# Attention with the heads of chunks 1 and 0 alternating, one sequence of other products, and x3 joined before its sum

## The chip, the cores and the metric

The kernel runs on one core of a Trainium2 chip. A core has a tensor engine (PE, matrix products and transposes, with a weight load PEld before each), a vector engine (DVE), a scalar engine (ACT), a GpSimd engine (POOL) and a sync engine (SP) on whose queue nearly all transfers are issued. Each runs its own list of instructions in order; they meet at semaphores. The metric is the device time of one execution in microseconds, as the median of several runs.

## The reference

A trunk of two layers over 2048 tokens of width 1024, in 32-bit floats. The first layer is a pooling mixer. Keys and values come from its result x2, once. The second layer, where the change lies, is:

```python
h = rms_norm(x, b_norm[j])
q, z = jnp.split(h @ b_w_in[j], 2, axis=-1)
o = stick_breaking_attention(q, k_sh, v_sh)      # 16 heads of 64
x = x + (o * jax.nn.silu(z)) @ b_w_out[j]        # x3
x = x + (p[i] @ ple_w[i]) * jax.nn.sigmoid(x @ ple_gate_w[i])
```

The attention weight of key s for query t is sigmoid(logit) times the product of (1 - sigmoid) over the keys between s and t: a running product along the keys, taken from the last key back, for all keys before the query.

## The kernel before, in words

A product in full precision is made of three passes: each operand is stored as a rounded high part and the rest, and high*high, high*rest and rest*high are summed in PSUM (`piecewise`, L882 to L890; L885, L887 and L889 are its three matmuls).

The tokens are four chunks of 512. The first part of the program (to 1364.5 us of the profile) does the first layer for chunks 0 to 3 in turn, and stores queries, keys and values by chunk in HBM, x2 as floats, and its two parts for chunks 0 to 2. The second part is attention, and the products that remain lie beside it.

Attention goes in slots. A slot (c, h, kc) is one head h, the queries of chunk c against the keys of chunk kc; it has four steps, one for each 128 queries. Slots run for c = 3, 2, 1, 0, in each for all 16 heads, in each for kc = c down to 0. A slot with kc = c is a diagonal one, whose four score tiles are 128, 256, 384 and 512 keys wide; the others are full. So chunk 3 has 64 slots, chunk 2 has 48, chunk 1 has 32 and chunk 0 has 16. Step n does three things for three different slots, in the loop at L1035: `turn`, transposes of the running products that were made six steps ago (L841), which ACT copies as high part (L844) and DVE completes by a subtraction (L845); `front`, the scores of this step (L816, L817), sigmoid on ACT (L820) and the running product as a scan on DVE (L825 diagonal, L828 full); `gather`, the product with the values of what was turned two steps ago (L853, L854).

The other products come from a generator, `filler`, of which each step takes `rate` matmuls (L1054 to L1057). During chunk 3's slots it is `gate_z` for chunks 3, 2, 1, 0: z = silu(x2 @ wz) to HBM, 192 matmuls for a chunk. During the slots of chunk c it is then `post(c + 1)`: the output product of the chunk just done, sum to x3 (L947), x3 in two parts (L951 on ACT, L952 on POOL), the gate product and that with the embedding p, and for each of eight tiles of 128 channels sigmoid (L974), multiplication (L978), the two parts of x3 added (L979, on POOL while attention runs, L980), four transposes (L986) and the store. 768 matmuls lie beside 256 steps of chunk 3, 432 beside 192, 128 and 64 steps. At the end of a chunk's heads what is left of the generator is run out, and a new one starts with a new rate (L1068 to L1075). `post(0)` runs last, alone: the tail.

`soon(k, fn)` puts work k steps later in the order. After a pair of heads is done, `gated` (L859) adds the end values, multiplies by z on POOL (L866); `pair_up` (L892) makes the two parts of it that the output product reads (`og`, L897, L898).

Most of the order is that of the source. A scheduler places the instructions on the engines and chooses buffers from the pools: 10 tiles for queries, keys and values, 18 for the pairs that products read, 6 for stored weights, 2 PSUM banks each for scores, turned tiles, sums and dense products.

## Time and profile before

| | |
|---|---|
| median of 3 runs | 2768.99 us (2768.77 to 2770.73) |
| the profiled execution | 2768.39 us |
| its span, first to last instruction | 2765.4 us |
| instructions | 39537 |
| granted clock of PE | 0.999 |

A row of a group names line, engine, operation, the tile written and those read, then count, busy time and mean duration. A row of the waits says who waited for whom, for how many microseconds in total, how many times, and the longest. A row of the windows has the stretch and its length, then for each engine that worked its busy time and number of instructions, then the granted clock of PE, the share of the DMA engines and GB/s. A row of the timeline has start and duration in microseconds; in brackets stands how long the engine was idle before it, and what ended that. Matmuls are pipelined: one of 512 columns shows about 0.39 us, and the next starts 0.23 after it.

### The profile page before, as it was taken

To read this page: it belongs to the slowest core of one execution; us is meant where nothing else is said; L and a number is where in the kernel's file an instruction comes from. 1 tells how busy PE (TensorE), PEld (TensorE's weight loads), DVE (VectorE), ACT (ScalarE), POOL (GpSimd) and SP (SyncE) were. 2 spreads that over 40 slices of the span, in tenths; PEclk is the share of its full clock that TensorE was granted. 3 is DMA by queue.
4 is the path that set the end of the run, shared out by engine and by line. 5 is a ranking of instruction groups with operands and counts; after the bars stand their busy time and mean duration, and the time that the engine had idled before them with its cause. 6 is when DMAs were issued, how large, how long until landed. Compare 5 with 4: busy or idle time off the path is not lost. (4 is left out here: it accounts for less than half of the span.)

```text
span 2765.4 us, 39537 instructions
## 1 busy us (share of the span) xinstructions
PE 2725.7 (99%) x13715; PEld 2260.4 (82%) x13715; DVE 1956.0 (71%) x2573; ACT 1385.5 (50%) x2801; POOL 873.7 (32%) x695
## 2 busy tenths in 40 slices
PE   9999999999999999999999999999999999999999
PEld 7888888888888888888888888887887778888877
DVE  6766535655357544565499999999999988996632
ACT  5444532445234542345356566666666655664521
POOL 2574338642475325753121111111110011112220
PEclk9999999999999999999999999999999999999999
DMA  8664696747946479445678565555555566668765
GB/s 293 236 196 171 218 325 204 225 148 253 347 148 227 163 249 318 136 145 170 191 254 278 180 217 170 169 161 178 169 159 162 159 200 200 188 204 264 249 209 160
DMA packets 335835, 573.21 MB, mean 207 GB/s; under 512 B 32462, under 2 KB 166638, under 8 KB 335636
## 3 DMA queue, kind: packets, MB, share of 16 engines
q1 hardware_dynamic: 330186, 563.03, 63.5%
q10 hardware_dynamic: 5450, 7.66, 0.9%
q8 instruction: 108, 1.77, 0.3%
q14 instruction: 91, 0.75, 0.1%
HBM read 430.01 MB, written 132.19 MB: 203 GB/s over the span
## 5 line engine op out<-in xcount | busy, mean ns | idle before, releaser
L844 ACT CAST at<-psa 128x512 fp32r<-128x512 f32 (+3 forms) x640 | 334.1, 522 | 478.4 <-PE psa L841 459.6
L536 PE MATMUL psd<-wpair,x 128*128 128x512 f32 x2304 | 544.0, 393 | 0.0
L828 DVE TENSOR_TENSOR_SCAN pp<-kap,pp,zeros 128x512 f32<-128x512 f32 x384 | 512.9, 1336 | 3.1 <-ACT kap L820 2.4
L536 PEld LDWEIGHTS psd<-wpair,x 128*128 128x128 f32 x2304 | 428.2, 188 | 86.2
L845 DVE TENSOR_TENSOR at<-psa,at 128x512 fp32r<-128x512 f32 (+3 forms) x640 | 381.0, 596 | 88.0 <-ACT at L844 84.9
L841 PE MATMUL psa<-ident,pp 128*128 128x128 f32 x2176 | 347.0, 275 | 17.2 <-DVE at L845 15.5
L820 ACT ACTIVATE kap<-psl 128x512 f32<-128x512 f32 (+3 forms) x640 | 344.9, 539 | 15.1 <-PE psl L817 12.0
L841 PEld LDWEIGHTS psa<-ident,pp 128*128 128x128 f32 x2176 | 262.9, 140 | 93.0 <-DVE at L845 38.8
L816 PE MATMUL psl<-kk,qa 128*128 128x512 f32 (+3 forms) x640 | 281.4, 440 | 0.0
L854 PE MATMUL pso<-at,vv 128*128 128x512 f32 (+3 forms) x640 | 235.1, 367 | 0.0
L817 PE MATMUL psl<-kk,qb 128*128 128x512 f32 (+3 forms) x640 | 233.0, 364 | 0.0
L853 PE MATMUL pso<-at,vv 128*128 128x512 f32 (+3 forms) x640 | 232.7, 364 | 0.0
L825 DVE TENSOR_TENSOR_SCAN pp<-kap,ahead 128x128 f32<-128x128 f32 (+3 forms) x256 | 219.8, 859 | 5.8 <-ACT kap L820 4.1
L131 PE MATMUL psd<-xp,wpair 128*128 128x512 f32 x512 | 201.9, 395 | 1.3 <-ACT xp L269 0.8
L132 PE MATMUL psd<-xp,wpair 128*128 128x512 f32 x512 | 200.5, 392 | 0.0
L133 PE MATMUL psd<-xp,wpair 128*128 128x512 f32 x512 | 200.1, 391 | 0.0
L113 DVE SCALAR_TENSOR_TENSOR wpair<-wraw,gains,wpair 128x512 fp32r<-128x512 f32 x192 | 169.7, 905 | 36.8 <-ACT wpair L112 36.1
L923 POOL TENSOR_TENSOR zr<-zr,sgz 128x512 f32<-128x512 f32 x32 | 58.8, 1836 | 368.2 <-ACT sgz L922 311.3
L112 ACT ACTIVATE wpair<-wraw,gains 128x512 fp32r<-128x512 f32 x192 | 135.0, 720 | 59.0 <-PE psd L536 32.3
L108 POOL TENSOR_TENSOR wpair<-wraw,wpair 128x512 fp32r<-128x512 f32 x99 | 145.5, 1485 | 59.7 <-ACT wpair L106 59.7
L853 PEld LDWEIGHTS pso<-at,vv 128*128 128x128 f32 x640 | 120.2, 188 | 26.9 <-ACT at L844 0.2
L854 PEld LDWEIGHTS pso<-at,vv 128*128 128x128 f32 x640 | 120.3, 188 | 25.9
(211 smaller groups left out, 5402.4 us busy)
## 6 DMA issues: line engine op xcount, KB each, us to landing
kk<-kd SPq DMA_DIRECT2D x320, 128.0 KB
vv<-vd SPq DMA_DIRECT2D x160, 256.0 KB
wraw<-in_w_kv_dram SPq DMA_DIRECT2D x128, 256.0 KB
wpair<-wzd SPq DMA_DIRECT2D x64, 512.0 KB
wpair<-wod SPq DMA_DIRECT2D x64, 512.0 KB
wpair<-wgd SPq DMA_DIRECT2D x64, 512.0 KB
wpair<-wu SPq DMA_DIRECT2D x48, 512.0 KB
wpair<-wi SPq DMA_DIRECT2D x36, 512.0 KB
```

The costliest lines, as they stand in the source:

```text
L131: T.matmul(ps, wst(units, kt, 0, c0), acts[kt][:, 0], start=(begin and kt == order[0]), stop=False)
L536: T.matmul(pss2[i], ck["x2"][kt][:, xh, tk], wst(ws, kt, wh, 0, W5), start=(kt == 0 and xh == 0 and wh == 0), stop=(kt == KT - 1 and wh == 1))
L816: T.matmul(ps[:, :w], qa[:, qs], kk[:, :w], start=True, stop=False)
L817: T.matmul(ps[:, :w], qb[:, qs], kk[:, :w], start=False, stop=True)
L820: A.activation(out=kp[:, r0:], in_=ps[:, :w], func=AF.Sigmoid, scale=-1.0)
L825: V.tensor_tensor_scan(out=pp[:, r0:][:, ::-1], data0=kp[:, r0:][:, ::-1], data1=ahead[:, r0:][:, ::-1], initial=1.0, op0=ALU.mult, op1=AL ...
L828: V.tensor_tensor_scan(out=pp[:, ::-1], data0=kp[:, ::-1], data1=zeros.to_broadcast([P, W5]), initial=st["carry"][j], op0=ALU.mult, op1=AL ...
L841: T.transpose(pt[:, j * P : (j + 1) * P], pp[:, r0 + kt * P : r0 + (kt + 1) * P], ident)
L844: A.copy(out=at[:, 0, cs], in_=pt[:, cs])
L845: V.tensor_tensor(out=at[:, 1, cs], in0=pt[:, cs], in1=f(at[:, 0, cs]), op=ALU.subtract)
L853: T.matmul(po[:, cs], vv[:, kt, :], at[:, 0, cs], start=(st["diag"] and kt == 0), stop=False)
L854: T.matmul(po[:, cs], vv[:, kt, :], at[:, 1, cs], start=False, stop=(st["last"] and kt == 3))
```

## The change

1. The slots run as (1, h, 1), (1, h, 0), (0, h, 0) for each head, then all of chunk 2, then all of chunk 3. Where a slot has the keys of the slot before, it takes its key and value tiles and loads none. Since two chunks are in work at once, each has its own tile for the sum of a pair of heads.
2. The generator is one for all of attention: z of chunks 0, 1, 2, then `post(0)`, z of chunk 3, `post(1)`, `post(2)`; `post(3)` is the tail. Its rate has two values, one to step 208 and one after, and full steps get 1.2 times the share of diagonal ones. Twenty matmuls are left over for the end of the loop.
3. x2's parts are stored for chunk 3 too, and `gate_z` reads them from HBM for every chunk; those of chunk 0 are loaded ahead of the last step of the first part.
4. A pair of heads whose z isn't there yet is gated later.
5. In `post`, POOL adds the two parts of x3 at the start of a tile's gate product (`xw`), DVE adds that after its multiplication, and the tile's transposes follow two steps later in place of one tile later. In the tail this takes one of DVE's three operations a tile away. p is loaded and turned in two halves within the output products.

Two places show what it moves. PE, where the first attention stage ends. Before, steps 257 to 259, the first of chunk 2 (`psl` scores, `pso` with the values, `psa` turned):

```order
L817 MATMUL psl<-kk,qb 128x128
L853 MATMUL pso<-at,vv 128x512
L854 MATMUL pso<-at,vv 128x512
L841 MATMUL psa<-ident,pp 128x128 x4
L816 MATMUL psl<-kk,qa 128x256
L817 MATMUL psl<-kk,qb 128x256
```

Now, steps 208 and 209, where z of chunk 2 ends and `post(0)` begins (`xz` is x2, `og` the gated heads):

```order
L822 MATMUL psl<-kk,qb 128x512
L899 MATMUL psd<-xz,wpair 128x512
L901 MATMUL psd<-xz,wpair 128x512
L858 MATMUL pso<-at,vv 128x512
L859 MATMUL pso<-at,vv 128x512
L846 MATMUL psa<-ident,pp 128x128 x4
L821 MATMUL psl<-kk,qa 128x512
L822 MATMUL psl<-kk,qb 128x512
L897 MATMUL psd<-xz,wpair 128x512
L899 MATMUL psd<-xz,wpair 128x512
L901 MATMUL psd<-xz,wpair 128x512
L897 MATMUL psd<-og,wpair 128x512
```

The dense products (`psd`) go on through the change of work; before, ten steps had none.

DVE and PE at an output tile. Before, on DVE, a tile's last sum in chunk 2, whose transposes PE has twelve steps (of one scan each) further on:

```order
L825 SCALAR_TENSOR_TENSOR pp<-kap_12823,ahead 128x512
L898 TENSOR_TENSOR og<-os,og 128x512
L845 TENSOR_TENSOR at<-psa,at 128x512
L828 SCALAR_TENSOR_TENSOR pp<-kap_12820,pp,zeros 128x512
L980 TENSOR_TENSOR sg<-sg,x_19035 128x512
```

Now, on DVE, the first tile of chunk 0, at step 275, and on PE its transposes, after the scores of step 277:

```order
L833 SCALAR_TENSOR_TENSOR pp<-kap_12854,pp,zeros 128x512
L1005 TENSOR_TENSOR sg<-psd,sg 128x512
L912 TENSOR_TENSOR og<-os,og 128x512
L1006 TENSOR_TENSOR sg<-sg,xw 128x512
L850 TENSOR_TENSOR at<-psa,at 128x512
L833 SCALAR_TENSOR_TENSOR pp<-kap_12855,pp,zeros 128x512
```

```order
L822 MATMUL psl<-kk,qb 128x128
L899 MATMUL psd<-x_17857,wpair 128x512
L901 MATMUL psd<-x_17857,wpair 128x512
L897 MATMUL psd<-x_18027,wpair 128x512
L1011 MATMUL psao<-ident,sg 128x128 x4
L858 MATMUL pso<-at,vv 128x512
```

The sum now follows its multiplication on the same engine with no POOL instruction between, and PE comes to the tile two steps after it.

The diff, cut to what the steps touch:

```diff
-                if s + 1 < NSUB:
-                    nc.sync.dma_start(out=x2p[s][o], in_=f(pr))
+                nc.sync.dma_start(out=x2p[s][o], in_=f(pr))
...
-                early["q"] = load_q(NSUB - 1, 0)
-                early["k"] = [load_k(NSUB - 1, 0), load_k(NSUB - 2, 0)]
+                early["q"] = load_q(1, 0)
+                early["k"] = [load_k(1, 0), load_k(0, 0)]
+                early["x"] = [load_x2(0, o) for o in range(KT)]
...
                 def gated():
+                    if (c, h2) not in gates:
+                        soon(2, gated)
+                        return
+                    soon(3, finished)
                     zt = t2.tile([P, W5], F32, tag="zt", name="zt", bufs=1)
...
+                def finished():
+                    assert len(outs[c]) == h2
+                    outs[c].append(os)
+
...
                     soon(3, gated)
-                    soon(6, lambda: outs[c].append(os))
...
                 T.matmul(ps, wst(units, kt, 1, c0), acts[kt][:, 0], start=False, stop=(kt == n - 1))
+                if behind:
+                    behind(kt)
                 yield
...
-            xs = chunk[c]["x2"] if c == NSUB - 1 else []
-            for o in range(len(xs), KT):
-                pr = pair("xz")
-                nc.sync.dma_start(out=f(pr), in_=x2p[c][o])
-                xs.append(pr)
+            xs = early.pop("x")
...
-                yield from piecewise(ps, wz, xs, 0)
+                def behind(kt):
+
+                    early.setdefault("x", []).append(load_x2(c + 1, kt))
+
+                yield from piecewise(ps, wz, xs, 0, behind if o == KT - 1 and c < 2 else None)
...
                     nc.sync.dma_start(out=zd[c][o], in_=zr)
+                    gates.add((c, o))
 
                 soon(1, silu)
-                if c == 0:
-                    pair_up(NSUB - 1)
+                if c < 3:
+                    pair_up(0)
+                if c == 2 and o < 2:
+                    pair_up(1)
 
         POSTZ = 8 * 24
-        POST = 8 * 24 + 8 * 31 + 2
+        POST = 8 * 24 + 8 * 31
...
-            pin = t2.tile([P, 4, PLE], F32, tag="pin", name="pin", bufs=1)
-            nc.sync.dma_start(out=pin, in_=p[1, 0, c * W5 : (c + 1) * W5, :].rearrange("(j q) n -> q j n", q=P))
-            x3, og = [], ogs[c]
+            x3, og, pt_ = [], ogs[c], []
+            assert len(outs[c]) == 8
...
                 wo = stored(wod[o])
+                if o in (2, 5):
+                    pin = t2.tile([P, 4, P], F32, tag="pin", name="pin", bufs=1)
+                    nc.sync.dma_start(out=pin, in_=p[1, 0, c * W5 : (c + 1) * W5,
+                                                     len(pt_) * P : (len(pt_) + 1) * P].rearrange("(j q) n -> q j n", q=P))
...
-            pt_ = []
-            for k in range(2):
...
-            yield
+                if o < 2 and 0 < c < NSUB - 1:
+                    pair_up(c + 1)
+                if o in (4, 6):
+                    k = len(pt_)
...
+                    pt_.append(pr)
             made()
             late = []
             for o in range(KT):
+                xw = t2.tile([P, W5], F32, tag="tmp", name="xw", bufs=4)
+                G.tensor_tensor(out=xw, in0=f(x3[o][:, 0]), in1=f(x3[o][:, 1]), op=ALU.add)
+                if c < NSUB - 1:
+                    pair_up(c + 1)
+                    if o == 0:
+                        pair_up(c + 1)
                 wg = stored(wgd[o])
                 wl = stored(wld[o])
...
                 V.tensor_tensor(out=sg, in0=pl, in1=sg, op=ALU.mult)
-                (V if tail[0] else G).tensor_tensor(out=sg, in0=sg, in1=f(x3[o][:, 1]), op=ALU.add)
-                summed = soon(2, lambda o=o, sg=sg: V.tensor_tensor(out=sg, in0=sg, in1=f(x3[o][:, 0]), op=ALU.add))
-
-                def finish(o=o, sg=sg, summed=summed):
-                    summed()
+                V.tensor_tensor(out=sg, in0=sg, in1=xw, op=ALU.add)
...
-                    A.copy(out=ot, in_=pt)
+                    stay(A.copy(out=ot, in_=pt))
...
-                if late:
-                    late.pop()()
-                late.append(finish)
-                if c:
-                    pair_up(c - 1)
+                if tail[0]:
+                    while late:
+                        late.pop()()
+                    late.append(finish)
+                else:
+                    soon(2, finish)
                 yield
-            late.pop()()
-            yield
-
-        def beside(c):
-
-            if c < NSUB - 1:
-                yield from post(c + 1)
-                return
-            for cz in range(c, -1, -1):
-                yield from gate_z(cz)
-
+            while late:
+                late.pop()()
+            if c == 0:
+                early["x"] = [load_x2(NSUB - 1, o) for o in range(KT)]
...
+        def beside():
+
+            for c in range(NSUB - 1):
+                yield from gate_z(c)
+            yield from post(0)
+            yield from gate_z(NSUB - 1)
+            for c in range(1, NSUB - 1):
+                yield from post(c)
...
-        for c in range(NSUB - 1, -1, -1):
+        for cs in ((1, 0), (2,), (3,)):
             for h in range(NH):
-                for kc in range(c, -1, -1):
-                    slots.append((c, h, kc))
-        active, filler, owed, head = {}, beside(NSUB - 1), 0.0, {}
+                for c in cs:
+                    for kc in range(c, -1, -1):
+                        slots.append((c, h, kc))
+        active, filler, owed, head, sums = {}, beside(), 0.0, {}, {}
         LAG_T, LAG_G = 6, 8
         AHEAD = 4
-        rate = POSTZ / 64.0 - AHEAD * LAG_T / 256.0
-        done = set()
+        SPARE = 20
+
+        share = [1.0 if n < 4 * len(slots) and slots[n // 4][2] == slots[n // 4][0] else 1.2
+                 for n in range(4 * len(slots) + LAG_G)]
+        turn_at = 3 * 4 * NH + LAG_G + 8
+        z_rate = (3 * POSTZ - AHEAD * LAG_T - 2) / sum(share[:turn_at])
+        rest_rate = (3 * POST + POSTZ - SPARE) / sum(share[turn_at:])
...
-                os = head["os"] if h % 2 else t2.tile([P, W5], F32, tag="os", name="os", bufs=9)
+                if h % 2 == 0:
+                    sums[c] = t2.tile([P, W5], F32, tag="os", name="os", bufs=10)
                 head.clear()
-                head.update(q=early.pop("q", None) or load_q(c, h), carry=[None] * 4, o=[], os=os)
-            kk = early["k"].pop(0) if early["k"] else load_k(kc, h)
-            active[i] = dict(head, c=c, h=h, k=kk, v=load_v(kc, h), diag=kc == c, last=kc == 0, a=[], at={})
+                head.update(q=early.pop("q", None) or load_q(c, h), carry=[None] * 4, o=[], os=sums[c])
+            if i and slots[i - 1][1:] == (h, kc):
+                kk, vv = active[i - 1]["k"], active[i - 1]["v"]
+            else:
+                kk = early["k"].pop(0) if early["k"] else load_k(kc, h)
+                vv = load_v(kc, h)
+            active[i] = dict(head, c=c, h=h, k=kk, v=vv, diag=kc == c, last=kc == 0, a=[], at={})
...
-            owed += rate + (AHEAD if n < LAG_T else 0)
+            owed += share[n] * (z_rate if n < turn_at else rest_rate) + (AHEAD if n < LAG_T else 0)
...
-            for c in range(NSUB - 1, 0, -1):
-                if len(outs[c]) == 8 and c not in done:
-                    done.add(c)
-                    for _ in filler:
-                        settle()
-                    filler = beside(c - 1)
-                    rate = POST / (64.0 * c - (LAG_G + 2 if c == 1 else 1))
-                    owed = 0.0
+        settle()
+        pair_up(NSUB - 1)
         settle()
         for _ in filler:
             settle()
         tail[0] = 1
-        for _ in post(0):
+        for _ in post(NSUB - 1):
```

More of the change, by code (lines that the diff above doesn't have):

```diff
@@ L63, in trunk_kernel @@
     x2d = [[dram.tile([P, W5], F32, name=f"x2d{s}_{o}") for o in range(KT)] for s in range(NSUB)]
[L64 removed]
+    x2p = [[dram.tile([P, 2, W5], F32, name=f"x2p{s}_{o}") for o in range(KT)] for s in range(NSUB)]
     zd = [[dram.tile([P, W5], F32, name=f"zd{s}_{o}") for o in range(KT)] for s in range(NSUB)]
@@ L174, in stored, with load_x2 @@
         return units
+    def load_x2(c, o):
+        pr = pair("xz")
+        nc.sync.dma_start(out=f(pr), in_=x2p[c][o])
+        return pr
     early = {"v": [], "s": []}
@@ L955, in post @@
                 x3.append(pr)
-            pt_ = []
-            for k in range(2):
-                pt = psa.tile([P, W5], F32, tag="psa", name="psap")
-                for j in range(4):
-                    T.transpose(pt[:, j * P : (j + 1) * P], pin[:, j, k * P : (k + 1) * P], ident)
-                pr = t2.tile([P, 2, W5], F32R, tag="ple", name="ple")
-                A.copy(out=pr[:, 0], in_=pt)
-                V.tensor_tensor(out=pr[:, 1], in0=pt, in1=f(pr[:, 0]), op=ALU.subtract)
-                pt_.append(pr)
-            yield
+                if o < 2 and 0 < c < NSUB - 1:
+                    pair_up(c + 1)
+                if o in (4, 6):
+                    k = len(pt_)
+                    pt = psa.tile([P, W5], F32, tag="psa", name="psap")
+                    for j in range(4):
+                        T.transpose(pt[:, j * P : (j + 1) * P], pin[:, j, :], ident)
+                    pr = t2.tile([P, 2, W5], F32R, tag="ple", name="ple")
+                    A.copy(out=pr[:, 0], in_=pt)
+                    V.tensor_tensor(out=pr[:, 1], in0=pt, in1=f(pr[:, 0]), op=ALU.subtract)
+                    pt_.append(pr)
             made()
```

7 lines of the change are left out of this document (4 added, 3 removed).

## The prediction

> **What bounds the kernel now.** I read the page's engine rows and slices first, then the windows over the attention part, then the waits of the tensor engine, then the timeline of single steps.
>
> ```profile
> PE 2725.7 (99%) x13715; PEld 2260.4 (82%) x13715; DVE 1956.0 (71%) x2573; ACT 1385.5 (50%) x2801; POOL 873.7 (32%) x695
> DVE  6766535655357544565499999999999988996632
> ...
> PEclk9999999999999999999999999999999999999999
> ```
>
> The tensor engine (PE) seems full, at full clock, and the vector engine (DVE) is full for just the middle of attention. Whether something is left to gain shows only by stage. The windows are chunk 3, chunk 2, chunk 1, chunk 0 (the four attention stages, in the order in which they run) and the tail; the second group of rows counts the instructions of L885, one of the three lines that issue the dense products.
>
> ```profile
> 1364.50:1866.10 501.60, 498.02 (x2710) 414.55 (x2709) 473.10 (x564) 300.71 (x599) 76.56 (x44) 1.00 0.65 204
> 1866.10:2215.40 349.30, 339.09 (x1881) 277.18 (x1880) 343.89 (x432) 226.63 (x467) 39.69 (x24) 1.00 0.55 166
> 2215.40:2470.50 255.10, 249.16 (x1389) 209.12 (x1388) 230.96 (x305) 154.17 (x336) 34.90 (x24) 1.00 0.65 196
> 2470.50:2638.10 167.60, 165.65 (x898) 140.12 (x897) 113.50 (x175) 84.25 (x204) 32.49 (x23) 1.00 0.80 246
> 2638.10:2765.40 127.30, 118.54 (x554) 96.94 (x552) 35.52 (x52) 26.78 (x53) 15.45 (x12) 0.99 0.59 186
> ...
> 1364.50:1866.10 501.60, 101.30 (x256) 48.13 (x256) 1.00 0.65 204
> 1866.10:2215.40 349.30, 54.02 (x136) 25.64 (x136) 1.00 0.55 166
> 2215.40:2470.50 255.10, 55.37 (x139) 26.17 (x139) 1.00 0.65 196
> 2470.50:2638.10 167.60, 58.43 (x146) 27.30 (x145) 1.00 0.80 246
> 2638.10:2765.40 127.30, 61.99 (x156) 29.32 (x156) 0.99 0.59 186
> ```
>
> The columns are time, then PE, weight loads, DVE, ACT, POOL. DVE is 98.5% busy in chunk 2 (343.89 of 349.3) and 68% in chunk 0 (113.5 of 167.6): the stages have different bounds. To see what PE loses in each, I price its work from the starts of one undisturbed full step (128 queries against 512 keys) in chunk 3.
>
> ```profile
> 1560.43 0.60 PE L841 MATMUL psa<-ident,pp 128*128 128x128 f32 x4
> ...
> 1561.10 0.39 PE L817 MATMUL psl<-kk,qb 128*128 128x512 f32 x1
> 1561.33 0.40 PE L889 MATMUL psd<-xz,wpair 128*128 128x512 f32 x1
> ...
> 1562.02 0.40 PE L853 MATMUL pso<-at,vv 128*128 128x512 f32 x1
> ...
> 1562.50 0.60 PE L841 MATMUL psa<-ident,pp 128*128 128x128 f32 x4
> ...
> 1562.54 1.27 DVE L828 TENSOR_TENSOR_SCAN pp<-kap,pp,zeros 128x512 f32<-128x512 f32 x1
> ```
>
> Transposes and scores take 0.90 (1560.43 to 1561.33), three dense products 0.69, so 0.23 each, and the two products with the values 0.48. A full step is 1.38 us of PE; a diagonal step, whose four tiles are 128, 256, 384 and 512 wide, 5/8 of that, 0.86; four transposes of an output tile 0.44. By stage, with dense products as three times the L885 count:
> - chunk 3: 192 full 265.0, 64 diagonal 55.2, 768 dense 176.6: 496.8, lost 4.8
> - chunk 2: 128 full 176.6, 55.2, 408 dense 93.8, 6 output tiles 2.6: 328.3, lost 21.0
> - chunk 1: 88.3, 55.2, 417 dense 95.9, 7 tiles and two loads of the embedding turned 4.0: 243.4, lost 11.7
> - chunk 0: 55.2, 438 dense 100.7, 4.4: 160.3, lost 7.3
> - tail: 468 dense 107.6, 11 tiles 4.8, 0.9: 113.3, lost 14.0
>
> That is 1342.1 of work and 58.8 lost. What ends PE's idle time over all of this is DVE (two rows of PE's weight loads and of PE itself):
>
> ```profile
> PEld psa L841 <- DVE at L845: 38.8, 70, 2.1
> ...
> PE psa L841 <- DVE at L845: 15.5, 30, 1.6
> PE psao L986 <- DVE sg L980: 7.2, 4, 2.4
> ```
>
> How much is lost follows the ratio of DVE's busy time to PE's price. Three quiet stretches give two more points and an edge: all windows and L885 counts again.
>
> ```profile
> 1740.10:1866.10 126.00, 124.64 (x675) 102.68 (x674) 122.31 (x146) 77.12 (x155) 15.57 (x10) 1.00 0.53 167
> 2249.00:2437.50 188.50, 187.98 (x1048) 158.88 (x1047) 172.47 (x227) 114.68 (x251) 27.04 (x18) 1.00 0.65 197
> 1430.20:1740.10 309.90, 309.80 (x1699) 259.45 (x1698) 292.48 (x351) 187.04 (x375) 46.10 (x25) 1.00 0.68 214
> ...
> 1740.10:1866.10 126.00, 24.07 (x61) 11.46 (x61) 1.00 0.53 167
> 2249.00:2437.50 188.50, 43.74 (x111) 20.71 (x110) 1.00 0.65 197
> 1430.20:1740.10 309.90, 61.39 (x155) 29.15 (x155) 1.00 0.68 214
> ```
>
> 1430 to 1740 is ten heads of chunk 3 (120 full, 40 diagonal steps): price 307.1, DVE ratio 0.95, lost 0.9%. 2249 to 2437 is twelve heads of chunk 1 (48 and 48): price 187.3, ratio 0.92, lost 0.6%. 1740 to 1866 is the last four heads of chunk 3 (48 and 16): 122.1, ratio 1.00, lost 3.2%. All of chunk 2: 328.3, ratio 1.05, lost 6.4%. The same two rows price DVE: less 0.65 for each instruction beside scan and subtraction (351 less 320 is 31; 227 less 192 is 35), 120 full and 40 diagonal steps are 272.3, 48 and 48 are 149.7; so 1.84 a full step and 1.28 a diagonal one.
>
> **The change part by part.**
>
> Stage A, the alternating heads of chunks 1 and 0 (64 full and 128 diagonal steps), has 530 dense products beside it by the order of after. PE's price: 88.3, 110.4 and 121.9, together 320.6. DVE: 117.8, 163.8 and 65 other instructions at 0.65, 42.3: 323.9, ratio 1.01. Between the points 1.00 and 1.05 that is 3.5% lost: 9.4 us on all but the first 32 steps. These cost 65.7 now (1364.5 to 1430.2) against a price of 67.6, since the first have no transposes or value products yet: -1.9. A: 7.5 lost.
>
> Stage B, chunks 2 and 3 (320 full, 128 diagonal): 441.6, 110.4, 1482 dense 340.9, 22 output tiles and 3 embeddings 12.3: 905.2. DVE: 588.8, 163.8, 139 others 90.4: 843.0, ratio 0.93. Lost 0.7%: 6.3. The stretch of chunk 2 without any dense product at its start, and the hunger of DVE after it, are gone; that is where 21.0 went.
>
> Output tiles. In after the transposes of a tile follow DVE's last sum by two steps; now by four to thirteen, but for the last tile of a chunk, which has two. The places with little room are those of the row above: 4 waits, 7.2 us, 1.8 each. There the last sum stands behind POOL:
>
> ```profile
> 2240.39 0.66 DVE L978 TENSOR_TENSOR sg<-psd,sg 128x512 f32<-128x512 f32 x1
> ...
> 2243.34 0.69 DVE L980 TENSOR_TENSOR sg<-sg,x 128x512 f32<-128x512 f32 x1 [1.09 <-POOL sg L979]
> ...
> 2244.17 0.63 PE L986 MATMUL psao<-ident,sg 128*128 128x128 f32 x4 [2.40 <-DVE sg L980]
> ```
>
> In after nothing stands between product and sum but, at some, an attention half (0.6): the 2.95 from 2240.39 to 2243.34 becomes 0.6 to 1.2, which would have met PE at about its time. In a full step the scan ends 2.71 after its scores begin (1561.10 to 1563.81); two more instructions end it at 3.96; PE comes to the tile at two steps and a part, 5.07. With 1.1 of room, 0.5 with the half, and a queue on DVE that comes and goes, I take 0.4 a tile: 8.8 for the 22 in stage B. The bounds are 0 (28 of the 32 now) and 1.8, which is 39.6.
>
> Changes of work inside B (chunk 0's products to z of chunk 3 to chunks 1 and 2) have no drain any more. What PE waited at two such places of now:
>
> ```profile
> 2247.64 0.55 PE L841 MATMUL psa<-ident,pp 128*128 128x128 f32 x3 [0.71 <-DVE at L845]
> ...
> 2497.57 0.63 PE L986 MATMUL psao<-ident,sg 128*128 128x128 f32 x4 [1.64 <-DVE sg L980]
> ```
>
> With the 2.40 above that is 4.75 at the ends of two chunks; I keep 3.0, between 0 and 4.8.
>
> Tail. The twenty spare products and what was still queued (484 dense in the tail by the order, 468 now) cover the gating of the last pair of heads, where PE now waits for a tile's sum and for the last attention half:
>
> ```profile
> 2653.64 0.63 PE L986 MATMUL psao<-ident,sg 128*128 128x128 f32 x4 [1.16 <-DVE sg L980]
> ...
> PE psdt L885 <- ACT og L897: 0.9, 1, 0.9
> ```
>
> That is -2.1. The sum of x3's halves, made by POOL (12 operations in 15.45 in the tail's row, 1.3 each) during the gate product (24 times 0.23, 5.5), leaves the very end:
>
> ```profile
> 2758.13 0.69 DVE L978 TENSOR_TENSOR sg<-psd,sg 128x512 f32<-128x512 f32 x1 [5.17 <-PE psd L889]
> 2758.86 0.69 DVE L979 TENSOR_TENSOR sg<-sg,x 128x512 f32<-128x512 f32 x1
> 2759.58 0.69 DVE L980 TENSOR_TENSOR sg<-sg,x 128x512 f32<-128x512 f32 x1
> ```
>
> One of three goes: -0.7 of the path that ends the program; the other seven sums of the tail were hidden by PE and save nothing. Lost in the tail: 14.0 - 2.8 = 11.2. In the loop POOL makes 24 sums as before and DVE two operations a tile as before.
>
> DMA. Eight stores of x2 halves (512 KB each) come into the end of the first part, eight loads more are made of them, and 32 key loads of 128 KB and 16 value loads of 256 KB fall away: equal bytes, and the DMA share there is 0.66 (0.53 to 0.80 in attention). No row of PE's waits names a load, so I take 0. With the cover gone a late load costs PE its landing, which the chain shows once:
>
> ```profile
> 2456.30 3.05 DMA ends<-ve
> ```
>
> The embedding in two halves and the extra buffers: 0, hidden alike.
>
> Sum: lost after 7.5 + 6.3 + 8.8 + 3.0 + 11.2 = 36.8 against 58.8; work equal (320.6 + 905.2 + 116.6 = 1342.4). The gain is 22.0 of the profiled execution's 2768.4, which is its span and 3.0 around it: 2746.4. The median of the runs, 2769.0, is 0.6 higher: **2747.0**.
>
> [...]
>
> **The rivals.**
>
> *Output tiles wait as the four did.* Two steps of room are what those had. 1.8 for 22 tiles is 39.6 instead of 8.8: 2778, slower. Against it: the POOL step in the middle is gone. From 1.4 a tile (0.4 + 22.0/22) no gain is left.
>
> *POOL holds up DVE in stage A.*
>
> ```profile
> L828 DVE TENSOR_TENSOR_SCAN pp<-kap,pp,zeros x384: 1262/1274/2331, 1373.8 to 2470.3; 128x512 f32<-128x512 f32 x192
> ```
>
> A scan that meets POOL takes up to 1.06 longer. Stage A has about 41 POOL operations in 330 us, chunk 3 has 44 in 502. If two in three of them cost DVE 1.06, its work is 353, and at chunk 2's 98.5% the stage takes 358, 30 more than in the sum (328): 2777. For it: the z multiplications of three chunks now lie beside short steps. Against: such meetings happen now too, so they are in part inside the 1.84 and 1.28. [...]
>
> *The unevenness stays within the stages.* Loss of 6.4% in A and 1.5% in B: 11 and 7 more, 2765, hardly faster. Half of that, 2756, is likelier.
>
> *Every stage runs as the quiet stretch of chunk 1.* 0.6% in A and B, no wait at tiles or changes: 58.8 - (1.6 - 1.9 + 5.4 + 11.2) = 42.5 gained, 2726.5.
>
> *A load comes late at each pair of heads*, since keys are held by two heads: 16 times 2 of the 3.05 us of a landing, 2779. Against it: the buffers are ten as now, and a pair of heads needs eight tiles where a head of chunk 3 needs ten.
>
> **How the numbers follow.** Chances: the sum as worked out, within 7 us, 0.5; the unevenness rival 0.2 (most of it about 2756, some over 2763); the even one 0.12; tiles 0.07; POOL 0.06; loads and anything else 0.05. Twice out of ten is left outside 2732 to 2766: below, most of the even rival; above, the three slow ones. Under 0.2% (5.5 us) no measurement of this kernel tells a change. Faster 0.80, same 0.08, slower 0.12.
>
> **What would show it.** Right: DVE's share between 0.90 and 0.98 in every stretch of attention, PE waiting for DVE's subtraction less than 20 us over attention in place of 54 (38.8 + 15.5); no stretch without dense products; the end of the loop to the last instruction shorter by 3 or so beside its 16 extra products. Wrong: waits for the tile's sum by the dozen, DVE over 98% in stage A, or PE waiting for keys, queries or weights.

## The result, and the profile after

The changed kernel takes 2772.69 us (2768.99 to 2776.78, 22 runs), the kernel before, beside it, 2768.49 us (2765.59 to 2770.73, 22 runs). The ratio is 1.0016, 95% interval 1.0010 to 1.0022: 0.16% slower, hardly more than nothing, where 0.8% faster was forecast. The profiled execution took 2772.5 us with a span of 2769.4.

The windows over the changed kernel, with the same columns as before, are stage A (heads of chunks 1 and 0), stage B (chunks 2 and 3) and the tail; the first row is the page's engine row.

```profile
PE 2726.0 (98%) x13715; PEld 2267.2 (82%) x13715; DVE 1966.1 (71%) x2565; ACT 1388.2 (50%) x2801; POOL 891.5 (32%) x703
...
1364.80:1699.30 334.50, 328.39 (x1863) 277.02 (x1863) 320.89 (x443) 222.36 (x506) 67.48 (x40) 1.00 0.76 230
1699.30:2639.30 940.00, 918.22 (x4984) 764.25 (x4983) 859.89 (x1034) 546.79 (x1106) 126.53 (x76) 0.99 0.55 175
2639.30:2769.40 130.10, 123.09 (x574) 101.06 (x572) 28.23 (x41) 24.22 (x44) 21.83 (x17) 1.00 0.58 186
```

| | price of PE's work | forecast | measured |
|---|---|---|---|
| stage A | 320.6 | 328.1 | 334.5 |
| stage B | 905.2 | 923.3 | 940.0 |
| tail | 116.6 | 127.8 | 130.1 |

Stage B carries 16.7 of the 25.4 us that are missing. It has the products and tiles that were priced (494 times three dense products, 22 tiles). DVE is 91% busy, the share that the sum had, though with 859.9 us of work where 843.0 were priced. The granted clock is 0.99. Its waits, PE's weight loads first, then PE itself:

```profile
PEld psa L846 <- DVE at L850: 26.0, 28, 3.3
...
PE psa L846 <- DVE at L850: 16.8, 17, 3.2
PE psao L1011 <- DVE at L850: 2.7, 2, 1.4
PE psao L1011 <- DVE sg L1006: 1.4, 2, 0.7
```

The output tiles (`psao`) themselves are waited for 4.1 us in all, half of what I had put there, and only 1.4 of it for the sum. What PE waits for is DVE's subtraction (L850), ahead of the next turned tile (`psa`), as long as 3.2 us at a time. The timeline shows how such a wait comes about, at a tile of chunk 1:

```profile
2317.62 0.60 PE L846 MATMUL psa<-ident,pp 128*128 128x128 f32 x4
2317.62 0.67 DVE L1006 TENSOR_TENSOR sg<-sg,xw 128x512 f32<-128x512 f32 x1
...
2318.20 0.68 DVE L850 TENSOR_TENSOR at<-psa,at 128x512 fp32r<-128x512 f32 x1
...
2318.57 0.58 ACT L849 CAST at<-psa 128x512 fp32r<-128x512 f32 x1
...
2318.74 1.29 POOL L875 TENSOR_TENSOR os<-os,zt 128x512 f32<-128x512 f32 x1 [18.57 <-ACT os L873]
...
2318.80 2.32 DVE L833 TENSOR_TENSOR_SCAN pp<-kap,pp,zeros 128x512 f32<-128x512 f32 x1
...
2319.45 0.60 PE L1011 MATMUL psao<-ident,sg 128*128 128x128 f32 x4
...
2320.00 2.18 POOL L991 TENSOR_TENSOR xw<-x 128x512 f32<-128x512 f32 x1
...
2321.04 1.68 DVE L912 TENSOR_TENSOR og<-os,og 128x512 fp32r<-128x512 f32 x1
...
2322.65 0.68 DVE L850 TENSOR_TENSOR at<-psa,at 128x512 fp32r<-128x512 f32 x1
...
2323.38 0.66 PE L846 MATMUL psa<-ident,pp 128*128 128x128 f32 x4 [3.16 <-DVE at L850]
...
2324.70 0.63 PE L899 MATMUL psd<-x,wpair 128*128 128x512 f32 x1
```

The turned tiles and the output tiles share two PSUM banks in turn. The tile turned at 2317.62 has one, the output tile at 2319.45 takes the other. The next turned tile then needs the bank of 2317.62 again, and stands until the subtraction of that very tile is done, at 2323.33. Without the output tile in between it would have needed the subtraction one step earlier, done at 2318.88. Meanwhile DVE is at its latest: behind the tile's multiplication and sum come a scan that lies beside POOL's gating and takes 2.32 in place of 1.28, and a subtraction of a pair of heads that lies beside POOL's join of x3's halves (L991) and takes 1.68 in place of 0.68.

After the wait the products are slow (0.63 in place of 0.40). The windows of two microseconds there hold PE's busy time and granted clock:

```profile
2320.00:2322.00 2.00, 0.22 (x3) 1.00 0.83 217
2322.00:2324.00 2.00, 0.62 (x5) 1.00 0.94 291
2324.00:2326.00 2.00, 2.00 (x8) 0.60 0.03 11
2326.00:2328.00 2.00, 2.00 (x9) 0.55 0.61 225
2328.00:2330.00 2.00, 2.00 (x12) 1.00 0.09 37
```

The clock is lower over two windows, which loses 2 times 0.40 and 2 times 0.45, 1.7 us. A finer window has it at 0.50 from 2324.4 to 2327.8, for 3.4 us. Stage B has three such stretches, at 1870, 2259 and 2324, each behind an output tile: 5.1 us. PE worked 1.02 us in the 3.4 us ahead of 2324.4, and its longest wait there was 3.16; what lowers the clock was not shown beyond that.

### The profile page after: what moved, and what is told of

The parts are those of the page before. It is cut to its first block, busy times and chain, and to the rows that moved or that the text cites. A ratio compares the mean times of both kernels' runs of the same rounds, so it can differ in the third digit from the quotient of the medians.

```text
span 2769.4 us, 39483 instructions
## 1 busy us (share of the span) xinstructions
PE 2726.0 (98%) x13715; PEld 2267.2 (82%) x13715; DVE 1966.1 (71%) x2565; ACT 1388.2 (50%) x2801; POOL 891.5 (32%) x703
## 4 chain that ended last, share of the span: by engine, by line
PE 85%; DVE 11%; issue 2%; ACT 1%; DMA 1%; POOL 0%; SPq 0%; ACTq 0%; DVEq 0%; POOLq 0%
PE psd L540 19%; PE psd L132 9%; PE psd L131 9%; PE psd L133 9%; PE psa L846 7%; PE psd L899 5%; PE psd L901 5%; PE psd L897 4%; DVE pp L833 4%; PE pso L859 4%; PE psl L822 3%; PE pso L858 3%; PE psl L821 3%; DVE at L850 2%; DVE pp L830 1%
## 5 line engine op out<-in xcount | busy, mean ns | idle before, releaser
L833 DVE TENSOR_TENSOR_SCAN pp<-kap,pp,zeros 128x512 f32<-128x512 f32 x384 | 514.8, 1341 | 5.8 <-ACT kap L825 4.9
L850 DVE TENSOR_TENSOR at<-psa,at 128x512 fp32r<-128x512 f32 (+3 forms) x640 | 383.7, 599 | 83.4 <-ACT at L849 79.4
L846 PE MATMUL psa<-ident,pp 128*128 128x128 f32 x2176 | 347.1, 275 | 21.9 <-DVE at L850 20.8
L846 PEld LDWEIGHTS psa<-ident,pp 128*128 128x128 f32 x2176 | 265.6, 141 | 92.6 <-DVE at L850 37.9
L830 DVE TENSOR_TENSOR_SCAN pp<-kap,ahead 128x128 f32<-128x128 f32 (+3 forms) x256 | 226.6, 885 | 4.6 <-ACT kap L825 3.6
L875 POOL TENSOR_TENSOR os<-os,zt 128x512 f32<-128x512 f32 x32 | 47.2, 1474 | 341.6 <-ACT os L873 281.4
L972 POOL TENSOR_TENSOR x<-xr,x 128x512 fp32r<-128x512 f32 x32 | 51.9, 1622 | 310.2 <-ACT x L971 310.2
L937 POOL TENSOR_TENSOR zr<-zr,sgz 128x512 f32<-128x512 f32 x32 | 58.4, 1826 | 262.1 <-ACT sgz L936 185.8
```

Of the source, the lines that this page charges most:

```text
L833: V.tensor_tensor_scan(out=pp[:, ::-1], data0=kp[:, ::-1], data1=zeros.to_broadcast([P, W5]), initial=st["carry"][j], op0=ALU.mult, op1=AL ...
L846: T.transpose(pt[:, j * P : (j + 1) * P], pp[:, r0 + kt * P : r0 + (kt + 1) * P], ident)
L850: V.tensor_tensor(out=at[:, 1, cs], in0=pt[:, cs], in1=f(at[:, 0, cs]), op=ALU.subtract)
```

## The experiments

These theories were put against each other; R came up only after the first four runs. R: output tiles cost PE through the two PSUM banks that they share with the turned tiles. P: POOL's join of the halves costs through the DVE instructions beside it. L or S: two steps, or the joined sum, are too tight by themselves. B and W: crowds of DVE instructions, or too much DVE work, whatever the form of the tile.

**The old sum in the loop (a1_oldsum).** The sum of part 5 and its early transposes are undone while attention runs; p is still loaded in halves.

```diff
-                G.tensor_tensor(out=xw, in0=f(x3[o][:, 0]), in1=f(x3[o][:, 1]), op=ALU.add)
...
-                V.tensor_tensor(out=sg, in0=sg, in1=xw, op=ALU.add)
+                    G.tensor_tensor(out=sg, in0=sg, in1=f(x3[o][:, 1]), op=ALU.add)
+                    summed = soon(2, lambda o=o, sg=sg: V.tensor_tensor(out=sg, in0=sg, in1=f(x3[o][:, 0]), op=ALU.add))
...
-                    soon(2, finish)
+                late.append(finish)
```

> The changed kernel with the sum of an output tile as before in the loop: POOL adds the low half, DVE the high half two steps later, the transposes come one tile later; the tail keeps the joined halves. Theory S (the joined sum and its early transposes are what eats the gain: of the 27.5 us that PE loses in chunks 2 and 3 in stalls over 0.2 us, 20 lie at tiles where the product's multiplication, the sum and a subtraction of a pair of heads stand together on DVE): 2755, 15 less than the changed kernel. Theory B (any crowd of DVE instructions stalls PE, since only two turned tiles fit in PSUM, whatever the sum's form): within 4 us of the changed kernel, 2769 to 2774.

Measured 2755.56 us (2754.96 to 2757.36), ratio to the kernel before 0.9956 (0.9943 to 0.9970): 17 less than the changed kernel. This is what theory S expected. The change without the new sum in the loop is worth 13 us; the new sum takes them away again. Stage A and the tail stay (334.9 and 131.0), stage B goes from 940.0 to 921.8:

```profile
1700.40:2622.20 921.80, 910.59 (x4981) 760.58 (x4980) 856.43 (x1034) 545.85 (x1106) 116.66 (x74) 1.00 0.58 178
```

**No join (a2_nopool), five steps (a3_lag5), a spread-out sum (a4_spread).** Each takes away something else at the tile: POOL's join, the closeness of the transposes, the closeness of DVE's two instructions.

```diff
-                G.tensor_tensor(out=xw, in0=f(x3[o][:, 0]), in1=f(x3[o][:, 1]), op=ALU.add)
-                V.tensor_tensor(out=sg, in0=sg, in1=xw, op=ALU.add)
+                V.tensor_tensor(out=sg, in0=sg, in1=f(x3[o][:, 0]), op=ALU.add)
```

> The changed kernel without the join of x3's halves: DVE adds the high half alone, the low half is left out of the output. Theory P (POOL's join, 32 times, lengthens what DVE does beside it: 16.0 us of lengthening at its 24 in attention): 8 to 16 less than the changed kernel, 2757 to 2764, and fewer drops of the clock. Theory B: the join costs little, 0 to 4 less, 2768 to 2772.

```diff
-                    soon(2, finish)
+                    soon(5, finish)
```

> The changed kernel with an output tile's transposes five steps behind its sum in place of two. Theory L (two steps are too few: PE waits 6.1 us at these transposes, and two of the three drops of the clock, 1.7 us each, follow such a wait): 6 to 10 less than the changed kernel, 2762 to 2766. Theory B: the wait moves to the turned tile behind it, 0 to 3 less, 2769 to 2772.

```diff
-                V.tensor_tensor(out=sg, in0=sg, in1=xw, op=ALU.add)
+                summed = soon(2, lambda sg=sg, xw=xw: V.tensor_tensor(out=sg, in0=sg, in1=xw, op=ALU.add))
...
-                    soon(2, finish)
+                    soon(4, finish)
```

> The changed kernel with DVE's sum two steps behind its multiplication, and the transposes four steps behind. Theory B (the crowd of three DVE instructions at a tile, 2.0 us in two steps, is what stalls PE): 8 to 12 less, 2760 to 2764. Theory P: the join on POOL is still there, so only the transposes' share is gained, 3 to 6 less, 2766 to 2769.

Measured 2758.04 (2756.86 to 2761.11), 2754.70 (2753.19 to 2755.93) and 2759.41 (2757.57 to 2765.67): 14.7, 18.0 and 13.3 less than the changed kernel. The first lies in theory P's range; the second gains far more than theory L had, the third a little more than theory B had. Stage B of the three, in this order:

```profile
1700.50:2628.40 927.90, 915.45 (x4984) 762.67 (x4983) 846.50 (x1034) 546.70 (x1106) 84.60 (x52) 1.00 0.58 177
...
1702.20:2624.20 922.00, 911.91 (x4981) 759.73 (x4980) 855.66 (x1034) 546.11 (x1106) 126.44 (x76) 1.00 0.58 178
...
1698.80:2626.50 927.70, 914.48 (x4980) 760.61 (x4979) 856.84 (x1034) 546.01 (x1106) 122.16 (x76) 1.00 0.58 177
```

Three different remedies each give back half or more of the 25.7 us between the measured time and the forecast, 46 in sum. So their gains overlap, which suggests that they act on one place. Theory L falls by its reason: all waits at these transposes were 6.1 us over the program, 3.4 of them for the sum, and five steps gave 18.0. With five steps DVE's busy time is the same within 5 us (855.7 against 859.9), and PE loses 18 us less in stage B: where the tile falls in DVE's work matters more than how much work there is.

**The tile in the scores' banks (c1_psl).** This takes away only the sharing. Two steps, the join and the crowd stay.

```diff
-                    pt = psa.tile([P, 4, P], F32, tag="psa", name="psao")
+                    pool, tag = (psa, "psa") if tail[0] else (psl, "psl")
+                    pt = pool.tile([P, 4, P], F32, tag=tag, name="psao")
```

> The changed kernel, still two steps behind, but the transposes of an output tile go to the scores' PSUM banks in place of those of the turned tiles. Theory R (the tile takes one of the two banks of the turned tiles; the next turned tile then needs the subtraction of one step back and not of two, just when DVE is late): most of the 18 us that five steps gave come back, 2756 to 2761. Theory H (PE stands at the tile's own transposes for the sum, and all behind it stands too): nothing changes, 2768 to 2773.

Measured 2750.31 (2748.95 to 2751.63), ratio 0.9934 (0.9921 to 0.9946): 22.4 less than the changed kernel, more than theory R expected. Theory H falls. Stage B, PE's largest waits in it, and the timeline at the same tile:

```profile
1702.30:2617.90 915.60, 910.42 (x4985) 760.76 (x4984) 855.79 (x1034) 546.50 (x1107) 126.89 (x76) 1.00 0.59 179
...
PE psa L846 <- DVE at L850: 2.3, 4, 1.1
PE psao L1012 <- DVE sg L1006: 1.9, 3, 0.9
...
2308.06 0.60 PE L846 MATMUL psa<-ident,pp 128*128 128x128 f32 x4
...
2309.25 2.30 DVE L833 TENSOR_TENSOR_SCAN pp<-kap,pp,zeros 128x512 f32<-128x512 f32 x1
...
2309.88 0.60 PE L1012 MATMUL psao<-ident,sg 128*128 128x128 f32 x4
...
2310.49 0.62 PE L846 MATMUL psa<-ident,pp 128*128 128x128 f32 x4
...
2313.11 0.68 DVE L850 TENSOR_TENSOR at<-psa,at 128x512 fp32r<-128x512 f32 x1
...
2313.84 0.66 PE L846 MATMUL psa<-ident,pp 128*128 128x128 f32 x4 [1.12 <-DVE at L850]
```

The scan is as long as before (2.30), POOL does the same (1.29 at L875, 2.21 at L991), but the turned tile behind the output tile starts at once at 2310.49, and the one after it waits 1.12, not 3.16. The clock stays up: 1.00 in stage B and 1.000 over the profiled execution, where the changed kernel had 0.99 and 0.998.

**No join, in the scores' banks (g1_psl_nopool).** The edits of c1_psl and a2_nopool together.

```diff
-                G.tensor_tensor(out=xw, in0=f(x3[o][:, 0]), in1=f(x3[o][:, 1]), op=ALU.add)
-                V.tensor_tensor(out=sg, in0=sg, in1=xw, op=ALU.add)
+                V.tensor_tensor(out=sg, in0=sg, in1=f(x3[o][:, 0]), op=ALU.add)
...
-                    pt = psa.tile([P, 4, P], F32, tag="psa", name="psao")
+                    pt = pool.tile([P, 4, P], F32, tag=tag, name="psao")
```

> Two steps behind, an output tile's transposes in the scores' banks, and no join of x3's halves on POOL: DVE adds the high half alone, the low half is left out of the output. With the turned tiles' banks in use the join cost 14.7 (2772.7 to 2758.0). Theory R (what POOL and DVE do at a tile reaches PE through those banks): with the scores' banks the join costs 0 to 4, 2746 to 2750. Theory P (POOL's join costs by itself, whatever the bank): again 10 to 15 less, 2735 to 2740.

Measured 2745.19 (2742.39 to 2747.13): 5.1 less than c1_psl, where the same edit gave 14.7 with the shared banks. So two thirds of what POOL's join cost went through the banks. The rest is near the 0 to 4 of theory R, a little above it.

**The kernel before, with part 5 alone (d1_before5), and with the scores' banks alone (d2_before_psl).** The first diff is d1's, the second d2's, both against the kernel before.

```diff
+                G.tensor_tensor(out=xw, in0=f(x3[o][:, 0]), in1=f(x3[o][:, 1]), op=ALU.add)
...
-                (V if tail[0] else G).tensor_tensor(out=sg, in0=sg, in1=f(x3[o][:, 1]), op=ALU.add)
-                summed = soon(2, lambda o=o, sg=sg: V.tensor_tensor(out=sg, in0=sg, in1=f(x3[o][:, 0]), op=ALU.add))
+                V.tensor_tensor(out=sg, in0=sg, in1=xw, op=ALU.add)
...
+                    soon(2, finish)
```

```diff
-                    pt = psa.tile([P, 4, P], F32, tag="psa", name="psao")
+                    pool, tag = (psa, "psa") if tail[0] else (psl, "psl")
+                    pt = pool.tile([P, 4, P], F32, tag=tag, name="psao")
```

> The kernel before with part 5 of the change alone: halves joined by POOL ahead, DVE's sum right behind its multiplication, transposes two steps later. Theories S and R (part 5 by itself costs what it takes from the change): 10 to 18 slower than before, 2779 to 2787. If it costs only beside the even sequence with its denser products: within 4 of before, 2765 to 2773.

> The kernel before with one edit: the transposes of an output tile go to the scores' PSUM banks while attention runs. Theory R (a tile in the turned tiles' banks costs PE at the next turned tile, before as well; 17 us of before's stalls over 0.2 us in chunks 2 to 0 stand at tiles): 8 to 14 less than before, 2754 to 2760. If before's stalls at tiles come from DVE being full there, whatever the bank: 0 to 3 less, 2765 to 2769.

Measured 2769.57 (2767.94 to 2772.12) with a ratio of 1.0004 (0.9995 to 1.0013), and 2764.98 (2764.12 to 2766.69) with 0.9988 (0.9979 to 0.9996). The first misses theories S and R and lies where the other expectation had it. The second, 3.6 less, misses theory R as well and lies at the edge of its rival. Chunks 2 and 1 of d1 and of d2, and PE's waits in d2's attention and tail:

```profile
1867.30:2219.30 352.00, 339.54 (x1881) 278.24 (x1880) 344.70 (x431) 226.80 (x467) 45.80 (x25) 1.00 0.54 165
2219.30:2476.80 257.50, 250.15 (x1394) 209.17 (x1393) 234.99 (x306) 154.85 (x338) 38.73 (x24) 1.00 0.65 195
...
1866.30:2215.20 348.90, 338.59 (x1881) 277.23 (x1880) 343.56 (x432) 226.70 (x467) 39.34 (x24) 1.00 0.54 166
2215.20:2468.40 253.20, 249.17 (x1389) 208.73 (x1388) 230.78 (x305) 154.13 (x336) 34.44 (x24) 1.00 0.66 198
...
PE psa L841 <- DVE at L845: 14.8, 27, 2.0
PE psao L987 <- DVE sg L980: 6.2, 4, 2.0
```

Part 5 costs these two chunks 2.7 and 2.4 (before: 349.3 and 255.1), 0.4 for each of the 14 tiles turned in them, and its shorter tail gives 2.2 back. In the changed kernel a tile costs 24.4 / 22 = 1.1 through the shared banks. In chunk 2 DVE is full anyway (344.70 of 352.00 in d1), and a wait of PE there would let DVE catch up, which was not tested; that chunk 1 loses so little beside much the same products was not settled. Sharing the banks costs the kernel before 3.6 us, and not 8 to 14. A likely reason is that its transposes come one tile later, when DVE has caught up: in that order the changed kernel with shared banks (a1_oldsum) took only 5.2 more than c1_psl. So in the changed kernel either remedy, other banks or later transposes, gives most of the loss back; why the same two things together cost the kernel before so little (d1) stays open.

**The heads one chunk after the other (c2_noalt).** On a3_lag5.

```diff
-        for cs in ((1, 0), (2,), (3,)):
+        for cs in ((0,), (1,), (2,), (3,)):
```

> Five steps as in the run before, and the heads of chunk 0 first, then those of chunk 1, not alternating. Theory E (alternating evens out stage A): 5 to 10 slower than with alternating heads, 2760 to 2765. The sum of DVE's work by stage (ratio to PE 1.03 for chunk 0 alone, 1.01 for chunk 1 alone, 1.01 for both alternating, at the rates of the changed kernel): no difference, 2752 to 2758.

Measured 2808.13 (2805.99 to 2811.17), 53 slower, and both expectations miss. Stages B are alike (922.7 and 922.0); chunk 0 and chunk 1 take 390.4 in place of 336.3. Chunk 0 alone, and PE's waits in it:

```profile
1366.30:1514.20 147.90, 127.58 (x610) 101.30 (x608) 102.90 (x155) 73.68 (x182) 26.50 (x19) 0.88 0.67 205
...
PE psa L846 <- DVE at L850: 10.5, 13, 1.9
PE psa L846 <- DVE pp L830: 5.2, 6, 1.5
```

DVE is busy for 70% of it, so the ratio of work isn't what bounds it. PE waits for scans (L830), which it does nowhere in the rows of the changed kernel's attention: with only a diagonal tile and 2.5 dense products, a step seems too short for six of them to cover the way from a score to its transposes. The granted clock is 0.88 in the mean, which alone loses some 17.7 of the 147.9 us (an estimate, 0.12 of it). Chunk 1 alone has one wait of 7.2 us more (`pso` for DVE at L882). Alternating matters, though not by evening out DVE's work.

**Scans that wait their turn (c3_elastic).** On a3_lag5: transposes eight steps behind, and scans put off while an estimate of DVE's queue is above 0.7 us.

```diff
-        LAG_T, LAG_G = 6, 8
+        LAG_T, LAG_G = 8, 10
...
-            if scan is not None:
-                scan()
+            while waiting and (debt[0] < LIMIT or len(waiting) > MOST or scan is None):
+                run, price = waiting.pop(0)
+                run()
+                debt[0] += price
```

> Five steps as before, transposes of the running products 8 steps behind in place of 6, and a scan waits up to three steps when an estimate of DVE's queue is over 0.7 us, so that the subtractions, which free the turned tiles' banks, come first. Theory B (crowds of DVE instructions stall PE through these subtractions, and scans have time to spare): half or more of the 25 us in stalls over 0.2 us goes, 2738 to 2748. Theory W (DVE has too much work over whole stretches): 2751 to 2757, no gain.

Measured 2760.63 (2756.89 to 2762.82), 6 slower than a3_lag5. In the profiled execution, whose span is 2755.3 against 2754.1, stage B is 919.9, 2 less than there, and the two added steps come back in the tail, 133.6 in place of 129.9. Neither theory's range holds: theory B's half of the stalls did not come back, and theory W's range ends at 2757. Why the other executions took longer than the profiled one was not settled.

**Two versions beyond (e1_best, f1_even).** e1 has all of attention's other transposes in the scores' banks, output tiles four steps behind, and in the tail a second buffer for the stored tile. f1 adds half of z of chunk 3 to stage A.

```diff
-                    soon(2, finish)
+                    soon(4, finish)
...
-                    ot = t2.tile([P, 4, P], F32, tag="ot", name="ot", bufs=1)
+                    own = "zt" if tail[0] and o % 2 else "ot"
+                    ot = t2.tile([P, 4, P], F32, tag=own, name="ot", bufs=1)
```

> The changed kernel with all of attention's other transposes (output tiles, embedding, end values) in the scores' banks, output tiles four steps behind their sum, and in the tail a second buffer for the stored tile, so that the last copy doesn't wait for the store before it. Theory R: the run with the scores' banks (2750) less its remaining 5.0 us of waits for the sum, of which 2 to 4 come back, less 1.1 at the very end: 2744 to 2748. If four steps give nothing on top: 2748 to 2751.

```diff
+            yield from gate_z(NSUB - 1, 0)
             yield from post(0)
-            yield from gate_z(NSUB - 1)
+            yield from gate_z(NSUB - 1, 1)
...
+        z_rate = rest_rate = (3 * POST + 4 * POSTZ - SPARE - AHEAD * LAG_T) / sum(share)
```

> The run before this one, and the first half of z of chunk 3 moved ahead of the output products of chunk 0, at one rate for all steps: about 80 dense products more in stage A, as many fewer in chunks 2 and 3. The ratio of DVE's work to PE's price goes from 1.01 to 0.97 in stage A and from 0.93 to 0.95 after. If loss follows that ratio, stage A loses 5 to 7 less and the rest 1 to 2 more: 2740 to 2744. If what is left are single crowds of DVE instructions: within 2 of the run before.

Measured 2749.96 (2747.86 to 2751.61) and 2748.10 (2745.87 to 2750.00), ratios 0.9932 (0.9920 to 0.9945) and 0.9926 (0.9913 to 0.9940). The first lies where "four steps give nothing on top" had it: four steps, and the other transposes in the scores' banks, gave nothing over c1_psl beyond the second buffer. The second buffer gave its 1.1: the last copy followed its transposes (first row below, of e1), where it had waited for the store ahead of it (second row, of the changed kernel). Stage A of f1, with 73 more products at 0.23, is priced at 337.4 and took 347.7: 10.3 lost, where e1 lost 336.3 - 320.6 = 15.7. Stage B lost 14.2 (902.6 against 888.4) in place of e1's 916.8 - 905.2 = 11.6. That is the sign and about the size that the ratio of DVE to PE gives; the times of e1 and f1 overlap, so that the 1.9 us between them isn't shown. The rows are the two copies, then stages A and B of e1, then of f1.

```profile
2745.96 0.59 ACT L1016 COPY ot<-psao 128x512 f32<-128x512 f32 x1 [1.35 <-PE psao L1013]
...
2765.56 0.58 ACT L1013 COPY ot<-psao 128x512 f32<-128x512 f32 x1 [2.41 <-DMA out_dram<-ot]
...
1366.80:1703.10 336.30, 329.05 (x1864) 276.63 (x1863) 322.40 (x443) 222.56 (x506) 67.80 (x40) 1.00 0.76 228
1703.10:2619.90 916.80, 909.59 (x4980) 760.31 (x4979) 855.44 (x1034) 546.23 (x1105) 126.18 (x76) 1.00 0.59 179
...
1362.80:1710.50 347.70, 342.51 (x1936) 290.69 (x1936) 319.49 (x445) 223.97 (x509) 71.88 (x43) 1.00 0.80 239
1710.50:2613.10 902.60, 896.14 (x4913) 748.86 (x4912) 850.45 (x1032) 544.14 (x1102) 128.70 (x73) 1.00 0.59 180
```

## Why the prediction was wrong

**The step that failed: "I take 0.4 a tile: 8.8 for the 22 in stage B".** It asked when PE would come to the tile's own transposes, and put too much there: that wait was 4.1 us. It did not ask what the tile takes from others, and so put that at nothing. It takes one of the two banks of the turned tiles, and so halves the room of the next one, two steps after a crowd on DVE. With the sharing gone (c1_psl) stage B took 915.6, 24.4 less: 1.1 a tile, where 0.4 was put. Of the 24.4 the three stretches of lower clock are 5.1; PE's waits at the tiles themselves fell only from 4.1 to 1.9. The rival that had tiles at 1.8 (2778) came nearer to the time, for a reason that was wrong as well: it had PE wait for the sum. No rival of mine was the banks. My sign for it, waits for the sum by the dozen, would have missed the case; the other sign showed it, since PE's weight loads wait 37.9 and PE 20.8 us for the subtraction over attention, 58.7 in sum and no less than the 54.3 of before. DVE's share, 0.96 in stage A and 0.91 in stage B, lay where I had it for a right forecast, and so told nothing.

**Reading the old waits by their row.** That 28 of 32 tiles cost nothing was read from the rows of `psao` alone. In the changed kernel the cost stands in the rows of `psa`: 16.8 us of PE in stage B, and 2.3 in c1_psl. In the kernel before, d2_before_psl puts the sharing at 3.6 us; PE's waits at `psa` fell by 0.7 there and those at `psao` by 1.2, so the rows account for only a part.

**The join.** In my sum POOL's join cost nothing in the loop, since POOL made as many sums before. No run tests that difference by itself with the banks apart: without the join 5.1 us are gained there (g1_psl_nopool against c1_psl), but that takes away a POOL operation that the kernel before has as well. DVE is busy 846.5 us in stage B without it (a2_nopool), 859.9 with it and 856.4 with the old sum on POOL (a1_oldsum), and I had priced 843.0.

**The evenness.** Right in the main. Apart from the tiles I had 905.2 + 6.3 + 3.0 = 914.5 for stage B, and c1_psl has 915.6. That they are so close is partly luck: no run measured the 3.0 for the changes of work, and DVE had more work than priced. With a1_oldsum the change without the new sum in the loop gains 13 us, with c1_psl the whole of it gains 18, near the 22.0 of the sum.

**Stage A.** 7.5 was too little: 13.9 lost. The first 32 steps took 58.4, with 110 dense products, 12 full and 20 diagonal steps priced at 59.1, so 0.7 under the price and not 1.9; the others lost 276.1 - 261.5 = 14.6, 5.6% in place of 3.5%. The line through the points of long stretches lies too low here, and f1_even, with more products, still lost 10.3 us (3.1%) at a ratio of 0.95; why was not settled. It isn't the POOL rival: DVE is busy 320.9 there, less than the 323.9 of the sum.

**The tail.** Its dense products are 483, where the order had 484, and PE's waits there fell from 4.4 (3.1 for sums, 0.9 for an attention half, 0.4 for a turned tile) to 2.0, by 2.4 against the 2.1 forecast. It is 130.1 and not 127.8 mainly because the products and transposes of chunk 3's last full steps fall into it, work that I had counted in stage B: PE is busy 9.3 us with them there, and was 7.0 with those of chunk 0's diagonal steps. The 0.7 "of the path that ends the program" is not there: the last copy starts 3.41 after DVE's last multiplication starts, before and now, since both times it waited 2.41 for the store of the tile before. I had not asked what was late next behind the transposes.

**Loads and weight loads.** Loads stayed hidden, as said: none is among the rows of PE's waits in stages A and B. The share of weight loads shows the loss as well: stage B stands at 764.25 / 940.0 = 81.3% in the changed kernel and at 760.76 / 915.6 = 83.1% in c1_psl, against 414.55 / 501.60 = 82.6% in chunk 3 and 140.12 / 167.60 = 83.6% in chunk 0 before.

## What to carry to other kernels

When an instruction moves in the order, ask which buffers it takes and who is next in that rotation, not only what it waits for: with two banks, an output tile between two turned tiles left the next one half the room, and the wait showed in the neighbour's row (16.8 us at `psa`, 4.1 at `psao`). A share of busy time below 1 says nothing on crowds; look at where the late moments lie, and put a user of a scarce buffer elsewhere. If several unlike remedies together give back more than the whole of a loss, look for one place at which they act, and test it by itself.

## What the runs showed of the hardware

PE's clock stood at 0.50 for 3.4 us from 2324.4 on; in the 4 us ahead of 2324 PE had worked 0.22 and 0.62 us. Behind a wait of 3.2 us another 1.7 were lost so. The mean clock differed from execution to execution: among the 22 runs of the changed kernel those with 0.999 took 2770.2 us in the mean (10 runs), those with 0.996 took 2775.2 (6 runs), and the 6 between them 2773.4. A scan of 1.28 us beside POOL's multiplication of 1.29 took 2.32, so it lost 1.04, most of the time of the other instruction. Of the changed kernel's 384 scans at L833, 41 took over 1.40, each beside a POOL operation; those beside none took at most 1.29.
